# First six projection jobs on an input centred by rows but not normalised: tokens loaded by quarters, the norm made during later jobs

## The chip, the cores and the metric

The kernel runs on one NeuronCore of one Trainium2 chip. The metric is device time in microseconds (us) of one execution; the kernel before was timed three times. Engines are named as the profile names them: PE (TensorE, matrix products), PEld (its weight loads), DVE (VectorE), ACT (ScalarE), POOL (GpSimd) and SP (SyncE, which here only issues DMAs). "Span" is the time from the first to the last instruction in the profiled execution.

## The reference, cut to what matters

One layer of a hybrid decoder, in fp32, on 304 token rows: 16 learned meta tokens, 256 prompt tokens and 8 samples of 4 tokens. The change touches the input LayerNorm and the first projections behind it.

```python
def _layernorm(x, g, b):
    mu = jnp.mean(xf, axis=-1, keepdims=True)
    var = jnp.mean(jnp.square(xf - mu), axis=-1, keepdims=True)
    return (xf - mu) * lax.rsqrt(var + LN_EPS) * g + b

xp = _layernorm(jnp.concatenate([meta, x_prompt], axis=1), ln0_g, ln0_b)
xs = _layernorm(x_sample, ln0_g, ln0_b)
...
proj = x @ w_in            # 2048 x 7168: q, zf, v, g (8 heads of 128), three conv groups of 1024
... # HGRN2 recurrence on q, zf, v, gated by g; short gated convolution on the other three
mix = jnp.concatenate([o_a, y_b], axis=-1) @ w_o
h = _layernorm(ALPHA * x + mix, ln1_g, ln1_b)
ff = (jax.nn.silu(h @ w_gate) * (h @ w_up)) @ w_down
out = _layernorm(ALPHA * h + ff, ln2_g, ln2_b)
```

## The kernel before, in words

All activations stand transposed: 128 channels on the partitions, the 304 tokens (T; L = 288 without the meta tokens) along the free axis, 16 blocks of channels. Every fp32 operand of a product is split into a rounded part `hi` and a remainder `lo`, and each product is three matmuls: hi·xh, hi·xl, lo·xh.

Weights come in *pieces* of 512 KB (4 blocks of 128 rows by 256 columns). A *job* is one projection to 256 output channels: 4 pieces, 16 steps k, and in each step 2 x 3 matmuls into two PSUM banks (lines 184 to 186, in `run_job`). SP loads a piece into one of five raw buffers (line 117); ACT casts it to `hi` (line 74) and DVE subtracts to get `lo` (line 75); early in the program the same two instructions carry line 56, that of a helper which keeps an engine's instructions in the order in which they are written. Five pairs of hi and lo buffers exist, so piece n can be split once PE is through with piece n-5, and SP can load into a raw buffer once the piece before it in that buffer is split.

The jobs run in a fixed order: z, v, q, g of heads 0 and 1 (jobs 1 to 4), the same of heads 2 and 3 (jobs 5 to 8), a convolution block (three jobs), and so on; then the output projection and the feed-forward. Between the steps `tick` emits a little of the side work: taking finished banks out of PSUM (`evac`), the recurrence (`scan_head`), the convolution. The scheduler of the framework then sets the order of each engine's queue; every engine runs its own queue strictly in order.

At the start all of the input is loaded (lines 325 to 332: meta tokens, then halves of the rows), then the first weight pieces. The statistics of the three row tiles (128, 128 and 48 rows) are made on DVE and ACT, the rows are normalised, PE transposes them block by block (`turn`, line 387, xT), and `settle` applies gain and bias and splits into xh and xl. Four blocks are prepared before job 1 (bank zb) begins; the others follow in its steps. Job 2 (bank vb) is the first without such work.

Of the kernel before, what the change touches and what calls it, by code (L numbers as in the profile page):

```python
# [10 lines left out]
F32 = mybir.dt.float32  # L11
# [8 lines left out]
H = 8  # L20
# [20 lines left out]
LEAD = 4  # L41
# [18 lines left out]
def hybrid_step(ctx: ExitStack, tc: tile.TileContext, io):  # L60
# [10 lines left out]
    vec, act, pe = (InOrder(tc, e) for e in (nc.vector, nc.scalar, nc.tensor))  # L71
# [40 lines left out]
    def load_ahead(i):  # L112
        while state["dma"] < min(len(pieces), i + AHEAD_DMA):
# [14 lines left out]
    def split_next(first=False):  # L128
# [4 lines left out]
        if first:  # L133
            for k in range(n):
                act.copy(out=hi[:, k], in_=raw[:, k])
                nc.gpsimd.tensor_tensor(out=lo[:, k], in0=raw[:, k], in1=hi[:, k].bitcast(F32), op=ALU.subtract)
        elif p < 8:
            split(raw, hi, lo, vec, act)
        else:
            split(raw, hi, lo)  # L140
        splits[p] = (hi, lo)
        state["split"] += 1

# [5 lines left out]
    def tick():  # L149
        for q in lanes.values():  # L150
# [18 lines left out]
    def run_job(rhs, n, name):  # L169
# [5 lines left out]
        for i, k in enumerate(ks):  # L175
# [5 lines left out]
            for m in range(nm):  # L181
                cs = slice(m * P, (m + 1) * P)
                o = banks[m][:, :n]
                nc.tensor.matmul(o, hi[:, i % kb, cs], xh, start=(i == 0), stop=False)  # L184
                nc.tensor.matmul(o, hi[:, i % kb, cs], xl, start=False, stop=False)  # L185
                nc.tensor.matmul(o, lo[:, i % kb, cs], xh, start=False, stop=(i == nk - 1))  # L186
# [9 lines left out]
    prow0 = const.tile([NP0, P], F32, name="prow0")  # L196
    prows = const.tile([NP1, P], F32, name="prows")
    pvec = const.tile([P, NP0 + NP1], F32, name="pvec")
    crows = const.tile([3 * H, P], F32, name="crows")
# [14 lines left out]

    ident = const.tile([P, P], F32, name="ident")
# [85 lines left out]
    def rstd_tok(pool, mv, n, w, tag):  # L301
# [6 lines left out]
        nc.scalar.activation(out=t[:n], in_=v[:n], func=AF.Sqrt)  # L308
        nc.vector.reciprocal(out=r[:n], in_=t[:n])
# [8 lines left out]


    with tc.tile_pool(name="x0", bufs=1) as x0p, tc.tile_pool(name="x0w", bufs=3) as x0w:  # L320
        rows = [P, P, T - 2 * P]
        xts = [x0p.tile([P, D], F32, name=f"xt{i}") for i in range(3)]
        HD = D // 2
        nc.scalar.preload_act_table_set("sqrt_and_others")
        nc.sync.dma_start(out=xts[0][:NMETA], in_=io["meta_tokens"])
        nc.sync.dma_start(out=xts[0][NMETA:, :HD], in_=io["x_prompt"][0, : P - NMETA, :HD])
        nc.sync.dma_start(out=xts[2][:NMETA], in_=io["x_prompt"][0, 2 * P - NMETA :])
        nc.sync.dma_start(out=xts[2][NMETA : NMETA + NS], in_=io["x_sample"].rearrange("b t d -> (b t) d"))
        nc.sync.dma_start(out=xts[0][NMETA:, HD:], in_=io["x_prompt"][0, : P - NMETA, HD:])
        for c in range(2):  # L330
            cs = slice(c * HD, (c + 1) * HD)
            nc.sync.dma_start(out=xts[1][:, cs], in_=io["x_prompt"][0, P - NMETA : 2 * P - NMETA, cs])
        load_rows(nc.sync, prow0, 0, ("ln0_g", "ln0_b"))
# [6 lines left out]
        nc.gpsimd.memset(epsb, LN_EPS)  # L340

        junk = x0p.tile([T - 2 * P, D], F32, name="junk")

        def bn(i, st, c):
            vec.bn_stats(out=st[:, c], in_=xts[i][:, c * 512 : (c + 1) * 512])

        def stat_tiles(i):
            return [x0p.tile([P, n], F32, name=f"{tag}{i}") for tag, n in (("mv", 2), ("v", 1), ("r", 1), ("t", 1), ("nmr", 1))]

        def rstd(i):  # L350

            n = rows[i]
            mv, v, r, t, nmr = (x[:n] for x in sts[i])
            act.activation(out=t, in_=mv[:, 1:2], func=AF.Sqrt, bias=epsb[:n])
            vec.tensor_scalar_add(out=v, in0=mv[:, 1:2], scalar1=LN_EPS)
            yield
            vec.reciprocal(out=r, in_=t)
            yield
            vec.scalar_tensor_tensor(out=t, in0=r, scalar=v, in1=r, op0=ALU.mult, op1=ALU.mult)
            yield  # L360
            vec.tensor_scalar(out=t, in0=t, scalar1=-0.5, scalar2=1.5, op0=ALU.mult, op1=ALU.add)
            yield
            vec.tensor_mul(out=r, in0=r, in1=t)
            yield
            vec.scalar_tensor_tensor(out=nmr, in0=mv[:, 0:1], scalar=-1.0, in1=r, op0=ALU.mult, op1=ALU.mult)

        def together(*gens):
            for _ in zip_longest(*gens):
                pass

        def norm_rows(i, c, eng):
            n = rows[i]
            mv, _, r, _, nmr = (x[:n] for x in sts[i])
            x = xts[i][:n, c * 512 : (c + 1) * 512]
            if eng is vec:
                eng.tensor_scalar(out=x, in0=x, scalar1=mv[:, 0:1], scalar2=r, op0=ALU.subtract, op1=ALU.mult)
            else:
                eng.activation(out=x, in_=x, func=AF.Identity, scale=r, bias=nmr)
# [3 lines left out]
        def turn(k, tiles):  # L382
            if k not in xT:
                xT[k] = bank("xT")
            for i in tiles:
                n = rows[i]
                nc.tensor.transpose(xT[k][:, i * P : i * P + n], xts[i][:n, k * P : (k + 1) * P], ident[:n, :n])

        xfs = {}

        def settle(k):

            if k < NB:
                b = xT.pop(k)
                xf = x0w.tile([P, T], F32, tag="xf", name="xf", bufs=4)
                vec.tensor_scalar(out=xf, in0=b[:, :T], scalar1=pcol("ln0_g", k), scalar2=pcol("ln0_b", k), op0=ALU.mult, op1=ALU.add)
                act.copy(out=xh[:, k], in_=xf)
                xfs[k] = xf
            if k:
                eng = vec if k % 4 == 1 else nc.gpsimd  # L400
                eng.tensor_tensor(out=xl[:, k - 1], in0=xfs.pop(k - 1), in1=xh[:, k - 1].bitcast(F32), op=ALU.subtract)

        sts = [stat_tiles(i) for i in range(3)]
        bn0, bn1 = (x0p.tile([P, 4, 6], F32, name=f"bn{i}") for i in range(2))
        s2, mv2, x2 = x0p.tile([P, 2], F32, name="s2")[: rows[2]], sts[2][0][: rows[2]], xts[2][: rows[2]]
        act.activation(out=junk, in_=x2, func=AF.Identity, accum_out=s2[:, 0:1])
        for c in range(3):
            bn(0, bn0, c)
        vec.tensor_scalar(out=mv2[:, 0:1], in0=s2[:, 0:1], scalar1=1.0 / D, scalar2=None, op0=ALU.mult)
        vec.tensor_scalar(out=s2[:, 0:1], in0=s2[:, 0:1], scalar1=-1.0 / D, scalar2=None, op0=ALU.mult)  # L410
        bn(0, bn0, 3)
        vec.bn_aggr(out=sts[0][0], in_=bn0)
        together(rstd(0))
        act.activation(out=junk, in_=x2, func=AF.Square, bias=s2[:, 0:1], accum_out=s2[:, 1:2])
        for c in range(2):
            norm_rows(0, c, act)
        for c in range(4):
            bn(1, bn1, c)
        vec.tensor_scalar(out=mv2[:, 1:2], in0=s2[:, 1:2], scalar1=1.0 / D, scalar2=None, op0=ALU.mult)
        vec.bn_aggr(out=sts[1][0], in_=bn1)  # L420
        together(rstd(1), rstd(2))
        pb = bank("pb", "main")
        nc.tensor.transpose(pb[:, :NP0], prow0, ident[:NP0, :NP0])
# [775 lines left out]
```

## Time and profile before

| | us |
|---|---|
| median of 3 runs | 1412.75 (1412.15 to 1412.88) |
| profiled execution, its own time | 1411.89 |
| its span | 1410.2 |
| PE busy in it | 1382.0 (98%) |
| DVE, ACT, POOL busy | 831.2, 587.9, 115.6 |
| first matmul of job 1 | 20.15 |
| first matmul of job 2 | 45.35 |
| first matmul of job 7 | 114.69 |

A row of the time view reads: start, duration, engine, line, operation, output<-inputs, shape, count, and in brackets the idle time of the engine ahead of it with what ended it. Rows that run back to back overlap a little in their durations, since matmul ends are modelled and vector instructions are pipelined; the distance from start to start is what an instruction costs its engine. The profiled time is 1.7 us longer than the span.

### The profile page before, as it was taken

Reading aid. Unit: us, or ns where it says so; the run is one execution under the profiler, and the core shown is the slowest. Engines: PE = TensorE matmul, PEld = TensorE weight load, DVE = VectorE, ACT = ScalarE, POOL = GpSimd, SP = SyncE. Lnnn points to the kernel's source line nnn. Section 1 sums busy time; section 2 is a strip of 40 time slices with the busy share of each in tenths; the row PEclk is TensorE's granted clock in tenths of the full one; section 3 lists DMA queues with packets and bytes.
Section 4 is the critical chain, followed back from the end, with each engine's and each line's share of the span. In section 5 each row is a group of like instructions: output and inputs, shape, how many; then the busy total and the mean of one; then the engine's idle time right before and its main releaser. Section 6 shows DMA issues by size and latency. Waiting matters only on the chain.

```text
span 1410.2 us, 24922 instructions
## 1 busy us (share of the span) xinstructions
PE 1382.0 (98%) x10311; PEld 1365.6 (97%) x10311; DVE 831.2 (59%) x1342; ACT 587.9 (42%) x823; POOL 115.6 (8%) x174
## 2 busy tenths in 40 slices
PE   5999999999999999999999999999999999999996
PEld 4999999999999999999999999999999999999995
DVE  6756676876676888966444444444444444465444
ACT  5645544555443444434333333333333333343330
POOL 5201121111000332000000000000000000020000
PEclk9999999999999999999999999999999999999998
DMA  6655655555545554555555555555555555565541
GB/s 188 208 162 162 181 167 168 173 150 169 170 148 165 161 161 151 177 165 165 165 165 165 167 152 167 166 167 181 165 165 165 165 165 165 165 196 165 157 128 68
DMA packets 223858, 231.12 MB, mean 164 GB/s; under 512 B 7756, under 2 KB 219576, under 8 KB 223546
## 3 DMA queue, kind: packets, MB, share of 16 engines
q1 hardware_dynamic: 220240, 218.54, 50.9%
q0 software_dynamic: 3312, 10.72, 2.7%
q8 instruction: 81, 1.33, 0.4%
q10 hardware_dynamic: 192, 0.26, 0.1%
q14 instruction: 33, 0.27, 0.1%
HBM read 222.34 MB, written 7.15 MB: 163 GB/s over the span
## 4 chain that ended last, share of the span: by engine, by line
PE 98%; DVE 1%; POOL 1%; issue 0%; DVEq 0%; ACT 0%; POOLq 0%
PE u L184 7%; PE g L184 7%; PE wd L186 7%; PE g L185 7%; PE u L185 7%; PE wd L185 7%; PE g L186 7%; PE u L186 7%; PE wd L184 7%; PE wo L186 2%; PE wo L185 2%; PE wo L184 2%; PE zb L184 2%; PE zb L185 1%; PE zb L186 1%; PE vb L184 1%
## 5 line engine op out<-in xcount | busy, mean ns | idle before, releaser
L75 DVE TENSOR_TENSOR lo<-raw,hi 128x1024 fp32r<-128x1024 f32 (+1 forms) x408 | 501.7, 1231 | 476.5 <-ACT hi L74 476.0
L74 ACT CAST hi<-raw 128x1024 fp32r<-128x1024 f32 (+1 forms) x408 | 421.3, 1033 | 635.5 <-PE u L185 162.6
L185 PE MATMUL wd<-al,hi 128*128 128x288 f32 x704 | 207.9, 295 | 0.0
L184 PE MATMUL wd<-ah,hi 128*128 128x288 f32 x704 | 207.8, 295 | 0.0
L186 PE MATMUL wd<-ah,lo 128*128 128x288 f32 x704 | 207.8, 295 | 0.0
L184 PE MATMUL g<-ygh,hi 128*128 128x288 f32 (+1 forms) x452 | 134.0, 296 | 0.0
L185 PE MATMUL u<-ygl,hi 128*128 128x288 f32 (+1 forms) x452 | 133.9, 296 | 0.0
L185 PE MATMUL g<-ygl,hi 128*128 128x288 f32 (+1 forms) x452 | 133.9, 296 | 0.0
L184 PE MATMUL u<-ygh,hi 128*128 128x288 f32 (+1 forms) x452 | 133.8, 296 | 0.0
L186 PE MATMUL g<-ygh,lo 128*128 128x288 f32 (+1 forms) x452 | 133.6, 296 | 0.0
L186 PE MATMUL u<-ygh,lo 128*128 128x288 f32 (+1 forms) x452 | 133.6, 296 | 0.0
L185 PEld LDWEIGHTS wd<-al,hi 128*128 128x128 f32 x704 | 132.3, 188 | 0.0
L186 PEld LDWEIGHTS wd<-ah,lo 128*128 128x128 f32 x704 | 132.2, 188 | 0.0
L184 PEld LDWEIGHTS wd<-ah,hi 128*128 128x128 f32 x704 | 132.1, 188 | 0.1
L186 PEld LDWEIGHTS u<-ygh,lo 128*128 128x128 f32 x452 | 85.4, 189 | 0.0
L184 PEld LDWEIGHTS g<-ygh,hi 128*128 128x128 f32 x452 | 85.3, 189 | 0.1
L186 PEld LDWEIGHTS g<-ygh,lo 128*128 128x128 f32 x452 | 85.3, 189 | 0.0
L185 PEld LDWEIGHTS g<-ygl,hi 128*128 128x128 f32 x452 | 85.3, 189 | 0.1
L185 PEld LDWEIGHTS u<-ygl,hi 128*128 128x128 f32 x452 | 85.3, 189 | 0.0
L184 PEld LDWEIGHTS u<-ygh,hi 128*128 128x128 f32 x452 | 85.3, 189 | 0.0
L186 PE MATMUL wo<-mh,lo 128*128 128x288 f32 x256 | 75.9, 296 | 0.0
L185 PE MATMUL wo<-ml,hi 128*128 128x288 f32 x256 | 75.6, 295 | 0.0
(391 smaller groups left out, 3132.3 us busy)
## 6 DMA issues: line engine op xcount, KB each, us to landing
raw<-in_w_in SPq DMA_DIRECT2D x112, 512.0 KB, 3.7
raw<-in_w_gate SPq DMA_DIRECT2D x88, 512.0 KB, 3.6
raw<-in_w_up SPq DMA_DIRECT2D x88, 512.0 KB, 3.6
raw<-in_w_down SPq DMA_DIRECT2D x79, 512.0 KB, 3.6
raw<-in_w_o SPq DMA_DIRECT2D x32, 512.0 KB, 3.6
s<-in_state_hgrn POOLq DMA_DIRECT2D x8, 512.0 KB, 5.5
out<-sn POOLq DMA_DIRECT2D x8, 512.0 KB, 4.4
raw<-in_w_down SPq DMA_DIRECT2D x15, 256.0 KB, 2.8
```

What stands on the lines that cost most here:

```text
L74: a.copy(out=hi, in_=src)
L75: v.tensor_tensor(out=lo, in0=src, in1=hi.bitcast(F32), op=ALU.subtract)
L184: nc.tensor.matmul(o, hi[:, i % kb, cs], xh, start=(i == 0), stop=False)
L185: nc.tensor.matmul(o, hi[:, i % kb, cs], xl, start=False, stop=False)
L186: nc.tensor.matmul(o, lo[:, i % kb, cs], xh, start=False, stop=(i == nk - 1))
```

## The change

The first six jobs (z, v, q, g of heads 0 and 1, z and v of heads 2 and 3) no longer read the normalised input. They read `mixh` and `mixl`: the rows minus a rough centre (the mean of the row's first 128 values), transposed, times the gain, split. Two more columns at the end of that operand carry the gain and the bias themselves, so that each job also gives W·gain and W·bias. `evac_raw` then makes the projection of the normalised input: bank times the row's 1/std, plus W·gain times minus mean/std, plus W·bias. The buffers `mixh` and `mixl` are those that later hold the mixer's output.

* Loads: the tokens come in four quarters of columns, and after each quarter SP loads one weight piece; a quarter of the short row groups (sample rows, the prompt's end, meta tokens) is issued by ACT, the remaining three quarters of them by POOL; the gains by POOL, ahead of everything.
* The third row tile is padded with zero rows, so that its transposes from block 4 on are 128 wide and not 48.
* PE gets three products of the identity at the start and one after the first transposes; their results are not used.
* The centring of the later quarters, formerly part of the normalising on DVE and ACT, lies partly on POOL. Row statistics (`bn_stats`, `row_sums`) are made inside job 1 and closed after it in `first_norm`, which also spreads 1/std and -mean/std over the partitions by six small products (rb).
* `normed_input` makes the normalised xh, xl, which job 7 and all later jobs read: for each of 16 blocks one add and one multiply on POOL, an affine copy on ACT, an add on DVE, a cast on ACT and a subtraction on DVE. It runs as a side lane during jobs 2 to 6.
* The look-ahead of the splits is 0 for job 1's pieces and then grows to 3, one piece at a time.

The queue of SP, the program's first rows. Before (xt_103, xt_104, xt_105 are the three row tiles):

```order
L325 DMA xt_103<-in_meta_tokens 16x2048
L326 DMA xt_103<-in_x_prompt 112x1024
L327 DMA xt_105<-in_x_prompt 16x2048
L328 DMA xt_105<-in_x_sample 32x2048
L329 DMA xt_103<-in_x_prompt 112x1024
L332 DMA xt_104<-in_x_prompt 128x1024 x2
L211 DMA prow_67<-in_ln_g 16x128
L211 DMA prow_67<-in_ln_b 16x128
L117 DMA raw<-in_w_in 128x4x256 x112
```

and in the change (xt_111, xt_112 are the first two row tiles, the third is not loaded by SP):

```order
L57 DMA xt_111<-in_x_prompt 112x512
L57 DMA xt_112<-in_x_prompt 128x512
L57 DMA raw<-in_w_in 128x4x256
L57 DMA xt_111<-in_x_prompt 112x512
L57 DMA xt_112<-in_x_prompt 128x512
L57 DMA raw<-in_w_in 128x4x256
L57 DMA xt_111<-in_x_prompt 112x512
L57 DMA xt_112<-in_x_prompt 128x512
L57 DMA raw<-in_w_in 128x4x256
```

The first weight piece stood behind nine loads and now stands behind two of SP's.

DVE's queue from the split (lo) of piece 11 to that of piece 12, the last of job 3 and the first of job 4, before (pieces are counted from 0):

```order
L75 TENSOR_TENSOR lo<-raw,hi 128x1024
L541 SCALAR_TENSOR_TENSOR c<-c,loglb,w_1043 128x304
L543 SCALAR_TENSOR_TENSOR b<-reset,c 128x304
L509 CAST vs_1000<-vT 128x2x32
L550 TENSOR_SCALAR el<-b 128x16
L510 TENSOR_TENSOR vs_1000<-vT,vs_1000 128x2x32
L551 TENSOR_TENSOR el<-b 128x256
L552 TENSOR_TENSOR el<-b 128x32
L556 TENSOR_TENSOR w_1100<-b 128x256
L75 TENSOR_TENSOR lo<-raw,hi 128x1024
```

and in the change, from the split of piece 10 to just behind that of piece 12:

```order
L76 TENSOR_TENSOR lo<-raw,hi 128x1024
L516 TENSOR_TENSOR xf<-xf,xw 128x304
L76 TENSOR_TENSOR lo<-raw,hi 128x1024
L76 TENSOR_TENSOR xl<-xf,xh 128x304
L516 TENSOR_TENSOR xf<-xf,xw 128x304
L797 COPY u<-vT_504 128x2
L798 TENSOR_TENSOR vT<-vT_504,xr 128x304
L76 TENSOR_TENSOR xl<-xf,xh 128x304
L76 TENSOR_TENSOR lo<-raw,hi 128x1024
L799 SCALAR_TENSOR_TENSOR vT<-xnm,u,vT 128x304
```

Between the splits now stand the norm (xf, xl, with POOL's work in xf ahead of each) and the correction of the banks (u, vT); the recurrence's rows (c, b, el) come some pieces later.

The diff, cut to its core:

```diff
-LEAD = 4
+NXC = 4
+NRAW = 6
+WARM = 3
...
     def ensure(i):
         load_ahead(i)
-        while state["split"] < min(state["dma"], i + 1 + min(AHEAD_SPLIT, max(1, i - 1))):
+        while state["split"] < min(state["dma"], i + 1 + min(AHEAD_SPLIT, max(0, i + 1 - NXC))):
...
+    load_rows(pool, prow0, 0, ("ln0_g", "ln0_b"))
...
+        for dst, src in small:
+            act.dma_start(out=dst[:, :XC], in_=src[:, :XC])
+        tc.keep_in_program_order(nc.scalar.preload_act_table_set("natural_log_exp_and_others"))
+        vec.memset(xts[2][NS : 2 * NS, XC:], 0.0)
+        vec.memset(xts[2][2 * NS :, XC:], 0.0)
+        for c in range(NXC):
+            cs = slice(c * XC, (c + 1) * XC)
+            sync.dma_start(out=xts[0][NMETA:, cs], in_=xin[: P - NMETA, cs])
+            sync.dma_start(out=xts[1][:, cs], in_=xin[P - NMETA : 2 * P - NMETA, cs])
+            load_to(c + 1)
         load_ahead(0)
+        for dst, src in small:
+            pool.dma_start(out=dst[:, XC:], in_=src[:, XC:])
...
+        for _ in range(WARM):
+            idle_product(4)
...
+        def row_centre(i):
+            m = cen[: rows[i], i : i + 1]
+            vec.tensor_reduce(out=m, in_=xts[i][: rows[i], :P], op=ALU.add, axis=mybir.AxisListType.X)
+            vec.tensor_scalar(out=m, in0=m, scalar1=-1.0 / P, scalar2=None, op0=ALU.mult)
...
         def settle(k):
+            b, g = xT.pop(k)[:, :T], pcol("ln0_g", k)
+            act.activation(out=mixh[:, k, :T], in_=b, func=AF.Copy, scale=g)
+            vec.scalar_tensor_tensor(out=mixl[:, k, :T], in0=b, scalar=g, in1=mixh[:, k, :T].bitcast(F32),
+                                     op0=ALU.mult, op1=ALU.subtract)
...
+        row_centre(0)
+        centre(0, 0, vec)
+        row_centre(2)
+        centre(2, 0, act)
+        row_centre(1)
+        centre(1, 0, vec)
         pb = bank("pb", "main")
+        pe.transpose(pb[:, :NP0], prow0, ident[:NP0, :NP0])
         vec.tensor_copy(out=pvec[:, :NP0], in_=pb[:, :NP0])
+        turn(0)
+        turn(1)
+        idle_product(2)
         settle(0)
...
         def first_rhs(k):
+            c, i = divmod(k, 4)
+            if i == 0:
+                for j in (2, 3):
+                    turn(k + j)
+                for j in (2, 3):
+                    settle(k + j)
+                if k == 0:
+                    for j, eng in ((0, vec), (1, act), (2, pool)):
+                        centre(j, 1, eng)
+                    load_rows(pool, prows, NP0, ("b_f", "lb_param", "gnorm_g", "ln1_g", "ln1_b"))
...
+            if i == 2:
+                if k < 8:
+                    for j in range(3):
+                        centre(j, c + 2, pool)
+                split_next()
...
+            if k in (13, 15):
+                next(sums)
+            return mixh[:, k], mixl[:, k]
...
+    def first_norm():
+        for i in range(2):
+            nc.vector.bn_aggr(out=mv[:, i], in_=bns[i])
+        r, nmr = rstd_tok(sp, mv, P, 3, "x")
+        yield 5
...
+    def normed_input():
+        for k in range(NB):
...
+            nc.gpsimd.tensor_tensor(out=x, in0=mixh[:, k, :T].bitcast(F32), in1=mixl[:, k, :T].bitcast(F32), op=ALU.add)
+            yield 1
+            nc.gpsimd.tensor_tensor(out=x, in0=x, in1=xr, op=ALU.mult)
+            nc.scalar.activation(out=w, in_=xnm, func=AF.Identity, scale=pcol("ln0_g", k), bias=pcol("ln0_b", k))
+            yield 1
+            nc.vector.tensor_add(out=x, in0=x, in1=w)
+            yield 1
+            split(x, xh[:, k], xl[:, k])
+            yield 1
...
+    def evac_raw(n, banks, out, tag, fn):
+        yield LAG
+        for j in range(2):
...
+            nc.vector.tensor_copy(out=u, in_=banks[j][:, n : n + 2])
+            nc.vector.tensor_mul(out=t, in0=banks[j][:, :n], in1=xr[:, T - n :])
+            nc.vector.scalar_tensor_tensor(out=t, in0=xnm[:, T - n :], scalar=u[:, 0:1], in1=t, op0=ALU.mult, op1=ALU.add)
+            fn(j, t, t, u[:, 1:2])
...
+    def project(t0, out, tag, fn):
+        raw = state["job"] < NRAW
+        if state["job"] == NRAW:
+            flush("norm")
+        n = T - t0
+        banks = run_job(centred_rhs(t0), n + 2, tag) if raw else run_job(xrhs(t0), n, tag)
+        side("evac", (evac_raw if raw else evac)(n, banks, out, tag, fn))
```

More of the change, by code (lines that the diff above doesn't have):

```diff
@@ L112, in load_ahead, with load_to @@
     def load_ahead(i):
-        while state["dma"] < min(len(pieces), i + AHEAD_DMA):
+        load_to(i + AHEAD_DMA)
+    def load_to(end):
+        while state["dma"] < min(len(pieces), end):
             p = state["dma"]
@@ L124, in ensure, with split_next, split_steps @@
         load_ahead(i)
-        while state["split"] < min(state["dma"], i + 1 + min(AHEAD_SPLIT, max(1, i - 1))):
+        while state["split"] < min(state["dma"], i + 1 + min(AHEAD_SPLIT, max(0, i + 1 - NXC))):
             split_next()
-    def split_next(first=False):
+    def split_next():
+        for _ in split_steps(state["split"] >= 8):
+            pass
+    def split_steps(whole):
         p = state["split"]
@@ L132, in split_next @@
         raw = blocks(raws.pop(p), p)
[L133 to L140, printed above, removed]
         splits[p] = (hi, lo)
         state["split"] += 1
+        if whole:
+            split(raw, hi, lo)
+            return
+        if p:
+            split(raw, hi, lo, vec, act)
+            return
+        for k in range(n):
+            split(raw[:, k], hi[:, k], lo[:, k], vec, act)
+            yield
     lanes = {}
@@ L149, in tick @@
     def tick():
-        for q in lanes.values():
+        for q in list(lanes.values()):
             if not q[0]:
@@ L195, in hybrid_step @@
     NP1 = 2 * NB + 4 * H
-    prow0 = const.tile([NP0, P], F32, name="prow0")
-    prows = const.tile([NP1, P], F32, name="prows")
+    s0x = ExitStack()
+    x0p = s0x.enter_context(tc.tile_pool(name="x0", bufs=1, side="right"))
+    prow0 = x0p.tile([NP0, P], F32, name="prow0")
     pvec = const.tile([P, NP0 + NP1], F32, name="pvec")
-    crows = const.tile([3 * H, P], F32, name="crows")
     cvec = const.tile([P, 3 * H], F32, name="cvec")
@@ L307, in rstd_tok @@
         nc.vector.tensor_scalar_add(out=v[:n], in0=mv[:n, :, 1], scalar1=LN_EPS)
-        nc.scalar.activation(out=t[:n], in_=v[:n], func=AF.Sqrt)
-        nc.vector.reciprocal(out=r[:n], in_=t[:n])
+        nc.scalar.activation(out=t[:n], in_=v[:n], func=AF.Ln)
+        nc.scalar.activation(out=r[:n], in_=t[:n], func=AF.Exp, scale=-0.5)
         newton(r[:n], v[:n], t[:n])
@@ L317, in hybrid_step @@
     xl = xp.tile([P, NB, T], F32R, name="xl")
-    with tc.tile_pool(name="x0", bufs=1) as x0p, tc.tile_pool(name="x0w", bufs=3) as x0w:
+    mixp = s1.enter_context(tc.tile_pool(name="mixp", bufs=1))
+    mixh = mixp.tile([P, NB, T + 2], F32R, name="mh")
+    mixl = mixp.tile([P, NB, T + 2], F32R, name="ml")
+    mh, ml = mixh[:, :, :L], mixl[:, :, :L]
+    mv = xp.tile([P, 3, 2], F32, name="mv")
+    bns = [xp.tile([P, NXC, 6], F32, name=f"bn{i}") for i in range(2)]
+    s2t = xp.tile([P, 3], F32, name="s2t")
@@ L321, in hybrid_step @@
+    with s0x:
         rows = [P, P, T - 2 * P]
+        prows = x0p.tile([NP1, P], F32, name="prows")
+        crows = x0p.tile([3 * H, P], F32, name="crows")
         xts = [x0p.tile([P, D], F32, name=f"xt{i}") for i in range(3)]
[L323 to L333, printed above, removed]
+        XC = D // NXC
+        xin = io["x_prompt"][0]
+        small = ((xts[2][NMETA : NMETA + NS], io["x_sample"].rearrange("b t d -> (b t) d")),
+                 (xts[2][:NMETA], xin[2 * P - NMETA :]), (xts[0][:NMETA], io["meta_tokens"]))
@@ L340, in hybrid_step @@
[L340 to L350, printed above, removed]
-            n = rows[i]
-            mv, v, r, t, nmr = (x[:n] for x in sts[i])
-            act.activation(out=t, in_=mv[:, 1:2], func=AF.Sqrt, bias=epsb[:n])
-            vec.tensor_scalar_add(out=v, in0=mv[:, 1:2], scalar1=LN_EPS)
+        warm = bank("warm", "main")
@@ new lines, in centre, with turn @@
+        def centre(i, c, eng):
+            n = rows[i]
+            x, m = xts[i][:n, c * XC : (c + 1) * XC], cen[:n, i : i + 1]
+            if eng is act:
+                eng.activation(out=x, in_=x, func=AF.Identity, bias=m)
+            else:
+                eng.tensor_scalar(out=x, in0=x, scalar1=m, scalar2=None, op0=ALU.add)
+        xT = {}
+        def turn(k):
+            xT[k] = bank("xT")
+            for i in (0, 2, 1):
+                n = rows[i] if k * P < XC else P
+                pe.transpose(xT[k][:, i * P : i * P + n], xts[i][:n, k * P : (k + 1) * P], ident[:n, :n])
@@ L356, in rstd @@
             yield
[L357 removed]
+            act.activation(out=junk, in_=x2, func=AF.Square, bias=s2[:, 2:3], accum_out=s2[:, 1:2])
+            vec.tensor_scalar(out=m2[:, 1:2], in0=s2[:, 1:2], scalar1=1.0 / D, scalar2=None, op0=ALU.mult)
             yield
[L359 to L361 removed]
@@ L362, in rstd @@
[L362 to L378, printed above, removed]
@@ L380, in hybrid_step @@
-        xT = {}
[L382 to L421, printed above, removed]
+        row_centre(0)
@@ L432, in hybrid_step @@
+        turn(1)
+        idle_product(2)
         settle(0)
+        gb0 = pvec[:, :NP0].rearrange("p (a b) -> p b a", b=NB)
+        split(gb0, mixh[:, :, T:], mixl[:, :, T:], vec, act)
+        first_split = split_steps(False)
+        next(first_split)
         settle(1)
-        norm_rows(1, 1, vec)
-        norm_rows(2, 1, act)
-        settle(2)
-        settle(3)
+        for _ in first_split:
+            pass
+        sums = row_sums()
         def first_rhs(k):
-            c = k // 2 + 2
-            if k % 2 == 0 and c < 4:
-                norm_rows(0, c, act)
-                norm_rows(1, c, vec)
-                norm_rows(2, c, vec)
-            if k + LEAD < NB:
-                turn(k + LEAD, (0, 1, 2))
-            if k + LEAD <= NB:
-                settle(k + LEAD)
-            return xh[:, k], xl[:, k]
@@ new lines, in first_rhs @@
+            if i == 2:
[3 more added lines that the diff above has]
+                split_next()
+                if k + 2 < NB:
+                    for j in (2, 3):
+                        turn(k + j)
+                    for j in (2, 3):
+                        settle(k + j)
+            if i % 2:
+                vec.bn_stats(out=bns[i // 2][:, c], in_=xts[i // 2][:, c * XC : (c + 1) * XC])
+            if k in (13, 15):
+                next(sums)
@@ L473, in hybrid_step, with centred_rhs @@
     nc.gpsimd.memset(vtm, 0.0)
+    xr, xnm = (sp.tile([P, T], F32, tag="cc", name=n, bufs=2) for n in ("xr", "xnm"))
+    def first_norm():
[3 more added lines that the diff above has]
+        yield 5
+        for dst, src in ((xr, r), (xnm, nmr)):
+            b = bank("rb")
+            for i in range(3):
+                nc.tensor.matmul(b[:, i * P : i * P + rows[i]], src[:, i : i + 1].broadcast_to([P, P]), ident[:, : rows[i]],
+                                 start=True, stop=True)
+            nc.scalar.copy(out=dst, in_=b[:, :T])
+        side("norm", normed_input())
+        yield 1
+    def normed_input():
+        for k in range(NB):
+            x = sp.tile([P, T], F32, tag="y", name="xf", bufs=2)
+            w = sp.tile([P, T], F32, tag="up", name="xw")
+            nc.gpsimd.tensor_tensor(out=x, in0=mixh[:, k, :T].bitcast(F32), in1=mixl[:, k, :T].bitcast(F32), op=ALU.add)
[6 more added lines that the diff above has]
+            split(x, xh[:, k], xl[:, k])
+            yield 1
+    def centred_rhs(t0):
+        return lambda k: (mixh[:, k, t0:], mixl[:, k, t0:])
     def xrhs(t0):
```

73 lines of the change are left out of this document (39 added, 34 removed).

## The prediction

> **What bounds the kernel now.** I read the page first, then what TensorE waited for, then its time view around job 1, where the change works.
>
> ```profile
> span 1410.2 us, 24922 instructions
> PE 1382.0 (98%) x10311; PEld 1365.6 (97%) x10311; DVE 831.2 (59%) x1342; ACT 587.9 (42%) x823; POOL 115.6 (8%) x174
> PE   5999999999999999999999999999999999999996
> PE 98%; DVE 1%; POOL 1%; issue 0%; DVEq 0%; ACT 0%; POOLq 0%
> ```
>
> ```profile
> PE pb L423 <- DMA prow<-in_ln_b: 13.2, 1, 13.2
> ```
>
> Only the first slice of 35 us and the last are not full, the chain of waits lies 98% on PE, and PE's one long wait is for the first loads. So the time is PE's work plus what PE loses at the start and the end; what the change is worth is read from where PE stands when job 7 begins, behind which both kernels do the same work. PE's time view:
>
> ```profile
> 20.15 0.85 PE L184 MATMUL zb<-xh,hi 128*128 128x304 f32 x2
> ...
> 23.60 0.46 PE L185 MATMUL zb<-xl,hi 128*128 128x304 f32 x1
> 23.85 0.46 PE L186 MATMUL zb<-xh,lo 128*128 128x304 f32 x1
> ...
> 24.87 0.90 PE L387 MATMUL xT<-ident,xt 128*128 128x128 f32 x3
> 25.70 0.62 PE L184 MATMUL zb<-xh,hi 128*128 128x304 f32 x1
> ...
> 28.20 0.41 PE L184 MATMUL zb<-xh,hi 128*128 128x304 f32 x1
> 28.72 0.30 PE L184 MATMUL zb<-xh,hi 128*128 128x304 f32 x1
> 28.86 0.30 PE L185 MATMUL zb<-xl,hi 128*128 128x304 f32 x1
> ...
> 31.08 0.40 PE L184 MATMUL zb<-xh,hi 128*128 128x304 f32 x1
> 32.02 0.57 PE L387 MATMUL xT<-ident,xt 128*128 128x128 f32 x3
> 32.52 0.55 PE L184 MATMUL zb<-xh,hi 128*128 128x304 f32 x2
> ...
> 40.78 0.27 PE L454 MATMUL pb<-ident,prows 64*128 64x64 f32 x1
> 42.21 0.41 PE L185 MATMUL zb<-xl,hi 128*128 128x304 f32 x1
> 45.35 0.30 PE L184 MATMUL vb<-xh,hi 128*128 128x304 f32 x1
> ...
> 114.69 0.29 PE L184 MATMUL qb<-xh,hi 128*128 128x288 f32 x1
> ```
>
> Four things stand here. Job 1 begins at 20.15, the input being loaded and normalised by then. Until 28.20 a product costs 0.253 us from start to start, then 0.139: PE ran at half rate for its first 8.05 us of dense work. At full rate a step with its three transposes takes 1.44 us. Job 2 begins at 45.35 and job 7 at 114.69, 69.34 us later. In those 69 us DVE has room:
>
> ```profile
> 45.35:114.67 69.32, 69.32 (x516) 68.60 (x515) 42.83 (x71) 34.54 (x53) 5.13 (x4) 1.00 0.67 199
> ```
>
> (the columns are length, then busy time of PE, PEld, DVE, ACT, POOL, the granted clock, DMA share and GB/s). DVE 42.8, ACT 34.5, POOL 5.1 of 69.3.
>
> **The change, step by step.** *First product.* What has to land first sets it (rows of the time view, of the DMA issues with the us to landing, of the windows).
>
> ```profile
> 6.06 1.29 DVE L56 BATCH_NORM_STATS2 bn<-xt 128x6 f32<-128x512 f32 x2 [6.06 <-DMA xt<-in_x_prompt]
> 16.87 0.53 DVE L56 TENSOR_SCALAR xt<-xt,mv,r 128x512 f32<-128x512 f32 x1
> prows<-in_b_f POOLq DMA_DIRECT2D x1, 4.0 KB, 5.2
> prows<-in_lb_param POOLq DMA_DIRECT2D x1, 8.0 KB, 5.8
> 0.00:5.00 5.00, 0.00 (x0) 0.00 (x0) 0.00 (x0) 1.28 (x1) 3.96 (x13) 1.00 0.70 163
> 5.00:10.00 5.00, 0.00 (x0) 0.00 (x0) 1.76 (x3) 1.97 (x2) 4.48 (x28) 1.00 0.93 241
> ```
>
> Before, 128 + 448 KB had landed at 6.06. Now the second quarter tile is complete after 224 + 256 + 128 KB, so about 6.0; sum, scale and centre on DVE (0.3, 0.15, 0.53) end at 7.0. The gains come by POOL in 5.2 and 5.8 us from issues at 0.8 and 1.5: 7.3, and through PE and a copy at 7.8. The first weight piece ends at 1120 KB, by the windows' rates (163 GB/s x 5 us = 815 KB, then 241) at 6.3 and a completion later, about 8. PE: six transposes at half rate from 7.55 (0.24 each: the three at 24.87 take 0.83, with a gap for the 48-row shape, which falls away), the idle product, six more, then the first product at 10.6; ACT and DVE have its operands by 9.8. Bounds: 9.3 (the second six transposes cost nothing) and 13.5 (the quarters land as late as half tiles did). I take **10.6**, 9.55 earlier.
>
> *Job 1.* Half rate lasts 8.05 us there and I keep it: four steps of 1.52 and six transposes of 1.45 take PE to 18.1. The quarters are ready: SP's second pair is complete at 1.6 MB, by the windows at 8.3 plus a completion, POOL's part (issued behind DVE's memsets at about 4, 5.2 to 7 us) by 12, needed at 13.7. DVE's centring of the second quarter waits for POOL's meta rows, and behind it stand statistics and the lo of piece 1, not needed before 18. On POOL seven small loads (0.5 each) stand ahead of the third quarter's centring, which ends at 19; PE transposes it at 20.7. Then twelve steps at 6 x 0.139 = 10.0 and five groups of six transposes at 0.157 (0.50 for the three at 32.02, less the other shape) = 4.7: the last product ends at 32.8. DVE has to do 12 of these 14.7 us (ten mixl of 0.46, three splits, six statistics), so it keeps up, barely. The small transposes (40.78 to 42.21, less two products) add 1.3: job 2 begins at **34.1, gain 11.25**. Bounds 31.5 and 38 (POOL's six centres of about 1 us each late by a group).
>
> *PE's new work*: six small products for rb, 0.9; two columns in 304 on 480 products of jobs 2 to 6, 0.4. The three identity products lie before 7 us, where PE waits anyway; without that cover they would cost under 3.
>
> *Behind job 1* ACT's queue carries, ahead of the cast of piece 5, what it did at leisure before:
>
> ```profile
> 8.03 1.91 ACT L56 ACTIVATE junk<-xt 48x2048 f32<-48x2048 f32 x1 [5.94 <-DMA xt<-in_x_sample]
> 11.64 1.99 ACT L56 ACTIVATE junk<-xt,s 48x2048 f32<-48x2048 f32 x1
> 43.10 1.28 ACT L273 ACT_TABLE_LOAD   x1
> ```
>
> From its last mixh at 30.4: sum 2.1, cast of piece 4 1.04, squares 2.2, table 1.28, the two chains of Exp and Ln with DVE between 0.9, cast of piece 5 1.04 = 38.95, its lo on DVE 40.1. PE wants it at 37.6: **2.5 lost**. The rb products stand in PE's queue just ahead of that step and wait for the same chain on DVE, which ends at 39.0; job 2's last three pieces wait behind them. Bounds 0.5 and 4.
>
> *Jobs 2 to 6, DVE.* The largest cost. How POOL's two-input operations meet DVE is shown in the output-projection stage:
>
> ```profile
> 467.05 0.45 DVE L811 SCALAR_TENSOR_TENSOR yc<-xh,wo 128x288 f32<-128x288 f32 x1
> 469.39 0.45 DVE L825 TENSOR_TENSOR yc<-yc,lnc 128x288 f32<-128x288 f32 x1
> 469.76 0.45 DVE L813 SCALAR_TENSOR_TENSOR yc<-xl,yc 128x288 f32<-128x288 f32 x1
> 469.98 0.89 POOL L838 TENSOR_TENSOR lns<-lns,yc 128x288 f32<-128x288 f32 x1 [1.19 <-DVE yc L825]
> 470.13 1.83 DVE L75 TENSOR_TENSOR lo<-raw,hi 128x1024 fp32r<-128x1024 f32 x1
> 470.89 1.74 POOL L839 TENSOR_TENSOR lnq<-lnq,lq 128x288 f32<-128x288 f32 x1
> 471.88 1.06 DVE L825 TENSOR_TENSOR yc<-yc,lnc 128x288 f32<-128x288 f32 x1
> 476.04 1.21 DVE L75 TENSOR_TENSOR lo<-raw,hi 128x1024 fp32r<-128x1024 f32 x1
> ```
>
> A split takes 1.21 alone and 1.83 when POOL adds, the next operation 1.06 for 0.45: each POOL operation of 288 columns takes 0.61 from DVE, 0.64 at 304. An operation that reads PSUM (line 811) passes untouched. DVE's queue, from piece 5's lo at 39.0: pieces 5 to 9 in a row until 45.0 (1.14 each, a little waiting for ACT); then up to piece 24, job 7's first: 15 splits 17.1; 15 adds xf and 15 subtractions xl at 0.39 (0.37 between the starts of 469.39 and 469.76, scaled) 11.7; the banks' correction (copy 0.1, multiply 0.40, add 0.44, z one more 0.42) 10.0; head 0's recurrence 8.8. Sum 47.6. One POOL product of 1024 columns, as in the row below, 1.7. Thirty POOL operations meet it, 0.64 each; some fall on operations that read PSUM (about 15% of DVE's time), so 16.3.
>
> ```profile
> L564 DVE TENSOR_TENSOR el<-k,el 128x16 f32<-128x16 f32 x1 | 1.9, 1911 | 0.0
> ```
>
> 45.0 + 47.6 + 1.7 + 16.3 = **110.6**. PE would want it at 34.1 + 69.3 + 1.3 + 2.5 = 107.2. So PE loses 3.4 more, spread over jobs 5 to 7, and job 7 begins at 110.6, not 114.69. Bounds: no loss (107.2), every POOL operation met in full (113.5). Behind job 7 the norm is over, DVE's rows per four pieces sum to 10 us against PE's 13, and nothing more is lost. ACT has 46 us of work in these 66.
>
> Sum: 1411.89 - 4.1 = 1407.8 for the profiled execution; the median of the runs shown lies 0.86 above it: **1408.7**.
>
> **The rivals.** *DVE keeps up*: POOL's work falls into DVE's pauses. For it: DVE is 26 us idle there before. Against: the sum leaves only 62.2 - 49.3 = 12.9 us of room for 19.2. It decides if under two thirds of the POOL operations meet DVE. Job 7 at 107.2, gain 7.5: **1405.3**.
>
> *The lock is longer*, the slower side: each POOL operation keeps DVE out for its whole length, not for 0.61. POOL's add ran from 470.13, when DVE's operation ended, to 470.87; scaled to 304 columns 0.78. All thirty meeting DVE: 45.0 + 49.3 + 23.4 = 117.7, 3.0 later than before: **1415.8**. It is slower than before from 0.68 us per operation on. For it: DVE's queue is full, so every operation waits. Against: the two rows with 0.61. The Trainium skill says this in its page SBUF — State Buffer, section SBUF: two separate sides: whichever starts first holds the shared port pair for the whole instruction and the other fully blocks. The rows agree that DVE blocks, and put it at 0.61 of 0.74.
>
> *The clock stays at half rate through job 1*, because PE's new start has gaps (after its identity products, before each group of transposes). From 18.1: 72 products x 0.253 + 30 transposes x 0.235 = 25.3 and not 14.7; everything behind is 10.6 later: job 7 at 121.2, **1419.3**. For it: it took 8.05 us before, not fewer. Against: that start had gaps too, and rose.
>
> **How the numbers follow.** Forecast 0.50, DVE keeps up 0.23, the longer lock 0.18, half rate 0.09. The likeliest case's own range, from job 1's bounds and those of DVE's sum, is 1405.5 to 1412.5. A measurement of this kernel tells 0.2% (2.8 us) from no change, so faster is below 1409.9 and slower above 1415.6. Of the forecast 0.28 is faster and 0.22 the same; of the lock 0.06 the same and 0.12 slower. Faster 0.28 + 0.23 = 0.51; same 0.22 + 0.06 = 0.28; slower 0.12 + 0.09 = 0.21. The range for 8 in 10 takes in keeping up and most of the lock: 1404 to 1417.
>
> **What would show it.** First product of job 1 near 10.6, and its rate halving its cost near 18; job 2 at 34; a wait of PE for piece 5's lo of some 2 us; DVE without a pause from 45 to 110, its splits at 1.8 where POOL works; job 7 near 110.6. If splits stay at 1.2 beside POOL, or DVE shows pauses of several us in jobs 4 to 6, the third step is wrong and the time is lower; if job 2 begins after 38, the first is.

## The result, and the profile after

The changed kernel takes 1420.26 us (median of 5 runs, 1417.42 to 1420.65) where the kernel before takes 1412.75 (5 runs, 1412.15 to 1414.05): 1.0049 times as long, 95% interval 1.0034 to 1.0064. It is slower by 7.5 us. The prediction said 1408.7 and gave slower 0.21. The profiled execution took 1420.08.

The page of the kernel after, in the same rows as before:

```profile
span 1418.4 us, 25107 instructions
PE 1389.0 (98%) x10331; PEld 1371.5 (97%) x10331; DVE 867.7 (61%) x1404; ACT 601.0 (42%) x853; POOL 151.0 (11%) x202
PE   7988999999999999999999999999999999999996
```

PE's first slice is fuller than before (7, not 5), but the next two are 9 and 8, then 8. What PE waited for up to 160 us (sum, times, longest):

```profile
PE kv L681 <- ACT kdt L665: 4.2, 1, 4.2
PE xT L57 <- POOL xt L57: 3.8, 3, 3.2
PE z L196 <- DVE lo L76: 3.6, 2, 3.1
PE warm L57 <- POOL ident masks.py:199: 3.3, 1, 3.3
PE xT L57 <- DVE xt L57: 1.4, 1, 1.4
PE rb L500 <- ACT hi L57: 1.0, 1, 1.0
```

Before, the one long wait was the 13.2 us for the first loads. It is gone, and in its place stand three waits of 3 to 4 us (kv, xT and z; the 3.3 us of the row "warm" lie ahead of the identity products, before the job has work). PE's time view shows where they fall:

```profile
11.81 0.39 PE L57 MATMUL zb<-mh,hi 128*128 128x306 f32 x1
12.04 0.30 PE L57 MATMUL zb<-ml,hi 128*128 128x306 f32 x1
12.18 0.31 PE L57 MATMUL zb<-mh,lo 128*128 128x306 f32 x1
...
20.85 0.33 PE L57 MATMUL xT<-ident,xt 128*128 128x128 f32 x1 [0.33 <-POOL xt L57]
24.40 1.27 PE L57 MATMUL xT<-ident,xt 128*128 128x128 f32 x5 [3.22 <-POOL xt L57]
...
25.73 0.46 PE L57 MATMUL zb<-ml,hi 128*128 128x306 f32 x1
25.98 0.46 PE L57 MATMUL zb<-mh,lo 128*128 128x306 f32 x1
...
37.99 0.41 PE L194 MATMUL vT<-mh,hi 128*128 128x306 f32 x1
...
94.91 0.41 PE L196 MATMUL z<-mh,lo 128*128 128x306 f32 x1 [3.15 <-DVE lo L76]
...
116.44 1.04 PE L681 MATMUL kv<-vt,kdt 128*128 128x128 f32 x4 [4.15 <-ACT kdt L665]
...
122.64 0.30 PE L194 MATMUL q<-xh,hi 128*128 128x288 f32 x1
```

Job 1 begins 8.3 us earlier than before (11.81 against 20.15), job 2 7.4 us earlier (37.99 against 45.35), job 7 8.0 us later (122.64 against 114.69). From job 7 to the end of the span it is 1295.7 us here and 1295.5 before: all of the loss lies between job 2 and job 7. Behind each of the three waits (behind the second from 1.3 us after its end) the products come 0.254 us apart (25.73 to 25.98) for about 3.4 us, and then 0.14 again: PE ran at half rate. Jobs 2 to 6 in one row of the windows:

```profile
37.99:122.50 84.51, 75.70 (x527) 73.91 (x526) 81.97 (x150) 54.38 (x93) 40.99 (x39) 0.96 0.54 161
```

They take 84.5 us instead of 69.3. PE is idle in 8.8 of them (the waits above), and busy 6.4 longer: half rate twice, the six small products, two columns. DVE is busy in 82.0 of 84.5 us (42.8 of 69.3 before) and POOL in 41.0 (5.1).

### The profile page after: what moved, and what is told of

Read it like the earlier page. It is cut to its first block, busy times and chain, and to the rows that moved or that the text cites. A ratio compares the mean times of both kernels' runs of the same rounds, so it can differ in the third digit from the quotient of the medians.

```text
span 1418.4 us, 25107 instructions
## 1 busy us (share of the span) xinstructions
PE 1389.0 (98%) x10331; PEld 1371.5 (97%) x10331; DVE 867.7 (61%) x1404; ACT 601.0 (42%) x853; POOL 151.0 (11%) x202
## 4 chain that ended last, share of the span: by engine, by line
PE 93%; DVE 4%; ACT 1%; POOL 1%; issue 1%; DMA 1%; DVEq 0%; ACTq 0%; POOLq 0%
PE u L194 7%; PE g L194 7%; PE wd L196 7%; PE g L195 7%; PE u L195 7%; PE wd L195 7%; PE g L196 7%; PE u L196 7%; PE wd L194 7%; PE wo L195 2%; PE wo L194 2%; PE wo L196 2%; PE xb L194 1%; PE cb L194 1%; PE gbb L194 1%; PE cb L195 1%
```

## The experiments

All medians are to be read beside the change's 1420.3; the kernel before measured 1412.0 to 1412.7 with them.

**Centring off POOL.** In job 1:

```diff
-                if k < 8:
-                    for j in range(3):
-                        centre(j, c + 2, pool)
...
+                elif k < 12:
+                    for j, eng in ((0, vec), (2, act), (1, act)):
+                        centre(j, c + 1, eng)
```

> The centring of the third and fourth quarter of the input goes from POOL (1.56 to 1.63 us a tile, behind seven small loads) to DVE (one tile of each quarter, 0.49) and ACT (two tiles, 0.72 each). Theory A, that POOL's centring made TensorE wait 3.2 us in job 1 and that this wait put the clock back to half rate for 3.4 us: no wait over 1 us at the third quarter, no half rate behind it, job 2 at 33.3 and not 37.99. As DVE's queue begins earlier by as much, the whole gains about as much: 1415.8 for the kernel with the change of 1420.3. Theory B, that DVE alone bounds jobs 2 to 6 and its queue does not begin earlier (it waits for weight pieces or for ACT's chain behind job 1): job 2 at 33 to 34, job 7 still near 122, 1420.

1415.22 us (11 runs, 1413.81 to 1417.33). What the edit takes away, in the time view and the groups of POOL up to 125 us in the kernel after:

```profile
14.07 1.57 POOL L57 TENSOR_SCALAR xt<-xt,cen 48x512 f32<-48x512 f32 x1 [9.29 <-DMA xt<-in_x_prompt]
...
19.22 9.75 POOL L57 TENSOR_SCALAR xt<-xt,cen 128x512 f32<-128x512 f32 x6
...
L57 POOL TENSOR_SCALAR xt<-xt,cen 128x512 f32<-128x512 f32 x4 | 6.2, 1561 | 0.0
```

Six tiles took 9.75 us: five of them 1.55 to 1.58 each, and the third, beside a split of DVE, 2.05. So the third quarter's three were through at 24.3. POOL began them only at 19.22: its centre of the second quarter waited for a load until 14.07, and the seven small loads stand between. With DVE and ACT in POOL's place PE does not wait for the third quarter (0.55 us for the fourth), and job 2 begins at 35.37:

```profile
35.37 0.41 PE L194 MATMUL vT<-mh,hi 128*128 128x306 f32 x1
```

That is not the 33.3 expected, mostly because in this execution PE ran at half rate from 16.0 to 19.4, behind a wait of 1.7 us for the second quarter. In the execution of the kernel with eight raw jobs (below), which is alike in job 1, it did not, and job 2 began at 32.55. The whole gained 5.0 us, so an earlier job 2 is passed on (theory A); the waits in jobs 5 and 6 stayed (2.6 and 4.2 us).

**Norm left out, first try.** The call of `normed_input` was taken out and two zero fills of `xh` and `xl` put on POOL behind `make_constants`.

> The 16 steps that make the normalised input in jobs 2 to 6 are left out (POOL's add and multiply, ACT's line and cast, DVE's add and subtraction); POOL fills the operands of the later jobs with zeros instead, so from job 7 on other numbers are multiplied in the same time. Theory A, that these steps load DVE (about 0.78 for its own two operations and 1.28 for POOL's two, 16 times 2.06 = 33 us) and so make TensorE wait in jobs 5 and 6: no wait over 1 us and no half rate between job 2 and job 7; job 7 at 38.0 + 69.3 + 2.5 = 109.8 and not 122.5, the whole 1408. Theory B, that the correction of the banks and the recurrence of head 0, which stay, make DVE late by themselves: job 7 at 116 or later, 1414 or more.

1414.73 us (10 runs), job 7 at 118.2: inside theory B's numbers, but not by its cause. PE waited 5.5 us, at rb in job 2; DVE and POOL in the time view of this kernel:

```profile
37.39 1.22 DVE L57 TENSOR_TENSOR lo<-raw,hi 128x1024 fp32r<-128x1024 f32 x1 [0.73 <-ACT hi L57]
...
40.19 4.88 DVE L318 TENSOR_SCALAR xv<-mv 128x3 f32<-128x3 f32 x1
...
36.48 4.18 POOL L470 MEMSET xh<- 128x4864 f32 x1
40.59 4.17 POOL L471 MEMSET xl<- 128x4864 f32 x1
```

The fill itself did it: a DVE operation on three columns stood until POOL's second fill was over. In jobs 3 to 6 no wait was left, but this run does not price the norm; a later one does.

**Norm's add and multiply on DVE.**

```diff
-            nc.gpsimd.tensor_tensor(out=x, in0=mixh[:, k, :T]..., in1=mixl[:, k, :T]..., op=ALU.add)
+            nc.vector.tensor_tensor(out=x, in0=mixh[:, k, :T]..., in1=mixl[:, k, :T]..., op=ALU.add)
             yield 1
-            nc.gpsimd.tensor_tensor(out=x, in0=x, in1=xr, op=ALU.mult)
+            nc.vector.tensor_tensor(out=x, in0=x, in1=xr, op=ALU.mult)
```

> POOL's add and multiply of each of the 16 steps are done by DVE. Theory A, that each of POOL's operations on 304 columns keeps DVE out for 0.64 us, more than the 0.39 that DVE takes to do it: DVE gains 32 times 0.25 = 8 us by doing 32 operations more; the waits of 3.15 and 4.15 in jobs 5 and 6 and the half rate behind them shrink or go; job 7 at 112 to 115, the whole 1410 to 1413. Theory B, that POOL's operations mostly passed beside DVE's and the lateness came from DVE's own work: 12.5 us more on DVE, job 7 near 130 and the whole 1428 or more.

1410.98 us (11 runs, 1408.64 to 1412.29): 9.3 us less, and below the kernel before (0.9988, 0.9979 to 0.9996). Groups of DVE from 40 to 122 us, then POOL's up to 125, in the kernel after:

```profile
L76 DVE TENSOR_TENSOR lo<-raw,hi 128x1024 fp32r<-128x1024 f32 x20 | 28.3, 1420 | 0.0
L76 DVE TENSOR_TENSOR xl<-xf,xh 128x304 fp32r<-128x304 f32 x16 | 10.6, 662 | 1.9 <-ACT xh L75 1.8
...
L513 POOL TENSOR_TENSOR xf<-xf,xr 128x304 f32<-128x304 f32 x16 | 18.7, 1173 | 2.1 <-ACT xr L502 1.0
L511 POOL TENSOR_TENSOR xf<-mh,ml 128x304 f32<-128x304 f32 x16 | 16.3, 1018 | 27.0 <-DVE xl L76 27.0
```

and DVE's in this one:

```profile
L76 DVE TENSOR_TENSOR lo<-raw,hi 128x1024 fp32r<-128x1024 f32 x23 | 28.0, 1216 | 0.9 <-ACT hi L75 0.9
...
L513 DVE TENSOR_TENSOR xf<-xf,xr 128x304 f32<-128x304 f32 x16 | 7.5, 468 | 0.0
L76 DVE TENSOR_TENSOR xl<-xf,xh 128x304 fp32r<-128x304 f32 x16 | 7.5, 468 | 2.2 <-ACT xh L75 2.2
```

A split is back at 1.22 (from a mean of 1.42), a subtraction at 0.47 (from 0.66). From the start of piece 5's split to the end of the norm's last subtraction DVE was busy 72.8 us in the change (42.60 to 117.44) and 67.9 here (40.84 to 110.87), though here it did 30 operations more at 0.39 from start to start, 11.6 us (the other two lie ahead of this stretch). Of the rest of its work it did about 0.2 us less, two small operations of the next head. So the 30 on POOL had cost DVE 4.9 + 11.6 - 0.2 = 16.3 us, 0.54 each. Handing them to POOL took more of DVE than doing them there.

**Idle products in the wait.** Ahead of the third quarter's transposes:

```diff
+                if k == 6:
+                    for _ in range(3):
+                        idle_product(4)
```

> Three idle products of the identity (0.82 each at full rate) are put on TensorE ahead of the transposes of the third quarter, into the wait of 3.22 us for POOL; they write a bank that nothing reads. Theory A, that a pause of about 3 us is what puts the clock back to half rate: the pause is then under 1 us, no half rate behind it (products from 25 on at 0.14 and not at 0.254), job 2 at 36.4 and not 37.99, up to 1.5 us less in the whole: 1418.8. Theory B, that the clock falls whatever TensorE does there: job 2 at 38.0 to 38.5, 1420.3.

1418.43 us (5 runs, 1417.25 to 1419.23).

```profile
22.07 2.73 PE L57 MATMUL warm<-ident 128*128 128x512 f32 x6
24.64 1.09 PE L57 MATMUL xT<-ident,xt 128*128 128x128 f32 x6
...
25.71 0.30 PE L57 MATMUL zb<-ml,hi 128*128 128x306 f32 x1
25.85 0.30 PE L57 MATMUL zb<-mh,lo 128*128 128x306 f32 x1
```

The quarter comes no earlier, but the products behind it run 0.14 apart at once and job 2 begins at 36.99, 1.0 us earlier; at job 7 it is 0.8 (121.81). The medians differ by 1.8, but the ranges overlap for the most part. That fits theory A, but one execution does not show it: in those of the norm on DVE and of the kernel without identity products at the start, waits of 2.8 and 3.0 us for the same quarter were not followed by half rate either.

**Norm left out, second try.** In `normed_input` only two ACT casts of `xnm` a step remain:

```diff
+            nc.scalar.copy(out=xh[:, k], in_=xnm)
+            yield 2
+            nc.scalar.copy(out=xl[:, k], in_=xnm)
+            yield 2
```

> The norm's arithmetic is left out once more, without the zero fill on POOL that held DVE: in each of the 16 steps ACT alone writes the two operands of the later jobs, as casts of one and the same row tile (0.44 each, in place of the 0.64 and 0.44 that it did there), so from job 7 on other numbers are multiplied in the same time; DVE's two and POOL's two operations of a step are gone. Theory A, that these load DVE until TensorE waits in jobs 5 and 6: no wait over 1 us there, job 7 at 38.0 + 69.3 + 2.5 = 109.8 and not 122.5, the whole 1408. Theory B, that what stays (the banks' correction, the recurrence of head 0, the place of its matrix products) makes TensorE wait by itself: job 7 at 115 or later, 1413 or more.

1407.68 us (4 runs, 1406.69 to 1408.08), job 7 at 110.7. What PE still waits for between 38 and 200 us is one row:

```profile
PE rb L500 <- ACT hi L57: 0.6, 1, 0.6
```

The norm's arithmetic therefore makes all the waits of jobs 5 and 6, and with their half rate costs 12.6 us. The banks' correction and head 0, which stay, fit in DVE's room.

**Both edits** (centring on DVE and ACT, add and multiply on DVE).

> Both edits that gained alone: the centring of the third and fourth quarter on DVE and ACT, and the norm's add and multiply on DVE. Theory A, that the two losses stand one behind the other (PE's late start of job 2, then DVE's late queue): the gains add, 1411.0 less 5.0 = 1406. Theory B, that DVE's sum of 67 us from piece 5's lo on bounds job 7 whatever starts before, or that the centring on DVE and ACT only moves the wait inside job 1: 1409 to 1411, no better than the norm on DVE alone.

1406.71 us (5 runs, 1406.27 to 1409.05): 0.9963 of the kernel before (0.9951 to 0.9976), 13.6 less than the change as it was. The gains add to 14.3 and nearly all of it came. Jobs 2 to 6 and their waits:

```profile
34.40:109.80 75.40, 72.16 (x527) 70.81 (x526) 73.17 (x174) 54.63 (x93) 5.66 (x7) 1.00 0.55 169
```

```profile
PE ktb L645 <- DVE kp L614: 1.7, 1, 1.7
PE rb L500 <- ACT hi L57: 0.8, 1, 0.8
PE vsb L567 <- DVE vs L559: 0.7, 1, 0.7
```

DVE is still full (73.2 of 75.4 us), but PE loses only 3.2 us to it.

**Keys' products later.** One number, ahead of `kv = bank("kv")`:

```diff
-        yield 1
+        yield 8 if h == 0 else 1
```

> One number: in head 0's recurrence the products that read the transposed keys (the wait of 4.15 us in job 6) stand eight steps of the job later in TensorE's queue instead of one, so 42 products of job 6, whose weight pieces are split by then (the last at 109.1), are no longer queued behind them. Theory A, that the wait is one of place, DVE's lateness reaching TensorE through ACT's queue, where the copy of the keys stands behind the norm's cast: no wait over 2 us there, no half rate behind it; job 7 near 117 to 118.5 and not 122.5, the whole 1415 to 1417. Theory B, that DVE's queue bounds job 7 by its pieces in any order: the wait comes back at the first piece of job 7 or at a later product of head 0, job 7 or the next job loses as much, 1419.5 to 1420.5.

1416.78 us (6 runs, 1414.99 to 1418.3), 3.5 less, at the upper end of what theory A gave.

```profile
114.02 0.29 PE L194 MATMUL q<-xh,hi 128*128 128x288 f32 x1
...
116.73 0.61 PE L681 MATMUL kv<-vt,kdt 128*128 128x128 f32 x4
```

The wait of 4.15 us is gone, and job 7 begins at 114.02 with DVE unchanged (piece 24 split at 114.4). Theory A had it at 117 to 118.5. It is 8.6 us earlier there than in the change, but only 4.7 are left at the end of the profiled execution: 1.1 us of products now lie behind that point, and PE waits 2.2 us more behind it than in the change, 1.7 of them for the keys of a later head; the other 0.6 is not accounted for. (The products behind the keys in job 6 are 24; the expectation's 42 was a miscount.) In the change these products waited for ACT, and ACT for DVE:

```profile
115.18 0.46 DVE L516 TENSOR_TENSOR xf<-xf,xw 128x304 f32<-128x304 f32 x1
...
115.67 0.44 ACT L75 CAST xh<-xf 128x304 fp32r<-128x304 f32 x1 [2.20 <-DVE xf L516]
116.03 0.37 ACT L665 COPY kdt<-ktb 128x256 f32<-128x256 f32 x1
```

The copy of the keys needed nothing from the norm; it stood behind the norm's cast in ACT's queue.

**No identity products at the start** (`WARM = 0`).

> The three identity products ahead of the first transposes are left out (nothing reads what they write). Theory A, that they are why job 1 began at full rate, and that the wait for the third quarter hides what the rate costs before it: first products at 0.254 for 3.4 or 6.9 us, TensorE at the third quarter's transposes 1.5 to 3 us later and waiting that much less; job 2 still at 37.5 to 38.5, the whole within 1 us of 1420.3. Theory B, that the rate in job 1 moves job 2 one for one: job 2 at 39.5 to 41, 1422 to 1423.5.

1420.09 us (4 runs, 1418.89 to 1421.32). Job 2 and the whole came as theory A had them:

```profile
14.66 0.46 PE L57 MATMUL zb<-ml,hi 128*128 128x306 f32 x1
14.91 0.46 PE L57 MATMUL zb<-mh,lo 128*128 128x306 f32 x1
...
25.46 0.76 PE L57 MATMUL xT<-ident,xt 128*128 128x128 f32 x5 [3.01 <-POOL xt L57]
...
37.49 0.41 PE L194 MATMUL vT<-mh,hi 128*128 128x306 f32 x1
```

Job 1 begins 2.5 us later, at half rate until 17.5, and the wait for POOL's third quarter hides it. That wait is hardly shorter than in the change (3.0 against 3.2), since the quarter itself came 1.1 us later in this execution; but no half rate followed it. So the early rate bought nothing that these runs show, in part by chance.

**Spreading the norm over eight raw jobs**, on top of both edits (`NRAW = 8`, two of the four `yield 1` in `normed_input` made `yield 2`), and **the transposes of the keys later**, on top of both edits (`yield 8 if h == 0 else 3` ahead of `ktb`).

> The kernel with both edits (centring off POOL, the norm's add and multiply on DVE), with eight raw jobs instead of six: each of the 16 steps of the norm now takes six steps of a job instead of four, and the query and gate banks of the second head pair are corrected too (four banks, about 0.95 us of DVE each). Theory A, that DVE's full queue from 50 to 110 us is all that is left to lose there: its load per job falls from about 12.5 to 10.5 us in jobs 3 to 6, TensorE's waits of 1.7 and 0.7 us go, and the whole is 1404 to 1405.5 where both edits alone gave 1406.7. Theory B, that the load only moves behind job 7, where the recurrences of heads 1 and 2 fill DVE: the same waits come later, 1406.5 to 1408.5.

> The kernel with both edits, and head 0's transposes of its keys eight steps of the job behind the products before them instead of three (one number). Theory A, that the wait of 1.7 us that is left for these keys is one of place: it goes, 1405 where both edits alone gave 1406.7. Theory B, that DVE is late by an amount that some later product pays in any order: 1406.5 to 1407.

1408.0 us (8 runs, 1406.04 to 1409.72) and 1408.68 (7 runs, 1407.33 to 1410.05): no better than both edits. The first is what theory B gave, the second lies above both theories. With eight raw jobs the wait for the keys is gone from job 6 and one comes in job 8:

```profile
135.50 0.69 PE L645 MATMUL ktb<-ident,kp 128*128 128x128 f32 x2 [2.00 <-DVE kp L614]
```

With the later transposes head 0 no longer waits for its keys. In its place PE waits at a later product of head 0, in job 7,

```profile
PE sb L686 <- DVE ats_b L672: 1.0, 1, 1.0
```

and 1.6 us in all for the keys of later heads, where both edits alone have no wait behind job 7 until the end. In these two runs, with DVE full, a wait that was moved was paid somewhere else; where the keys' products were moved in the change itself, 3.5 us of it stayed gained.

## Why the prediction was wrong, step by step

* **First product.** 11.81 and not 10.6, within its bounds. From there PE ran at full rate, where half rate until 18.1 was forecast. PE came to the third quarter's transposes at 20.5, where 20.7 was forecast, but by luck: the full rate made up for the later start and for 1.6 us of waits for the second quarter.
* **Job 1: wrong, two sizes.** The step that failed is "POOL's six centres of about 1 us each", held to be in time, and with it POOL's part of the loads, forecast "by 12". That part was there at 14.07, and the four centres that end with the third quarter took 6.7 us instead of 4 (the seven loads 3.6, as forecast). So the third quarter was ready at 24.3 and not 19, where PE wanted it at 20.5. The wait cost 3.2 us, and the half rate behind it about 1.0 more at job 2. Job 2 began at 37.99, just inside the bound of 38, not at 34.1; without that centring on POOL the change takes 1415.2.
* **Behind job 1.** The wait for piece 5 and the chain of Exp and Ln was 1.05 us, where 2.5 stood.
* **DVE's sum was right.** 71.6 us from the start of piece 5's split to the end of piece 24's were forecast (38.95 to 110.6), 72.1 were measured, 2.0 of them idle, which the sum did not have. POOL's operations cost DVE 0.54 each on the mean, where 0.64 for 85% of them stood, which is 0.54 as well, and a split that met one took 1.86, where 1.8 stood. Piece 24 was split at 114.7 instead of 110.6 because the queue began 3.6 us later.
* **Job 7 at the end of DVE's queue: wrong, and the largest error.** Job 7 came 12.0 us after its forecast, 4.1 of them with the end of DVE's queue and 7.9 behind it. The sum took the split of piece 24 to be the only thing PE wants from DVE, "3.4 more, spread over jobs 5 to 7". PE also stands in order behind everything of head 0 that goes through DVE or ACT. It waited 3.15 us for piece 19 at 91.8 and 4.15 at 112.3 for the keys, with 24 products of job 6 behind them whose piece was split; job 7 began 7.9 us after piece 24 was ready. With the keys' products eight steps later and DVE's queue as it was, job 7 did begin when piece 24 was split, 114.0, as the step had assumed.
* **The rate behind a wait was left out.** Half rate was weighed for job 1's start alone. Here it came back after each of the three long waits, some 3.4 us at half rate each time. Such a stretch loses half its length, so by this estimate a wait of 3 us was worth up to 4.7.
* **The rivals.** DVE did not keep up. The longer lock gave 1415.8, nearer the measured time, for the wrong reason: the mean price of a POOL operation was 0.54, below the 0.68 from which it decides. Half rate all through job 1 did not come.

The idea of the change was sound: job 2 begins 7.4 us earlier, and with two placements changed the kernel takes 1406.7, 0.37% less than before. It was slower as made because it put work on POOL that was late there in job 1 and took DVE's time in jobs 2 to 6.

## What to carry to other kernels

When an engine's queue is full, look at every instruction in the bound engine's queue that depends on it, directly or through a third engine's queue, and not only at the last one: the first that is late stops all that is behind it. Price work that goes to POOL by what it takes from DVE as well as by its own time; here 0.54 us of DVE for an operation that DVE does in 0.39. And count a wait of PE of about 3 us or more with the half rate that follows.

## What the runs showed of the hardware

* **The rate after a pause.** In the first 200 us every pause of PE of 3.2 us or more between products in these runs (3.22, 3.3, 4.15, 4.2, 5.5, 5.6, 5.6) was followed by a granted clock of 0.50, for 3.4 us or twice that. Pauses of 1.7 to 3.15 were followed by it in some executions and not in others: 1.7, 2.6, 2.8 and 3.15 each at least once were and at least once were not. The rate in the first us of job 1 differed as well between executions of kernels that are alike there, full in the change's and half until 17 us in another. The Trainium skill describes this in its page TensorE: Matmul & The Clock Gate, section Part 1: The HAM clock gate: the rate follows from a free-running window of about 3.4 us. The lengths of 3.4 and 6.8 us agree, and so does the chance in between.
* **POOL and DVE hold each other up both ways.** A POOL operation on 128x304 took 1.02 and 1.17 us beside a full DVE, where 0.78 was scaled from the rows before. In job 1 a centre on POOL and a split on DVE that met took 2.05 and 1.91, where 1.56 and 1.21 are usual. The page SBUF — State Buffer of the Trainium skill (section SBUF: two separate sides) says that a POOL fill, which reads nothing, does not meet a DVE operation with two inputs, but meets one in a two-port performance mode. The run with the two fills agrees in the first, since the split passed at 1.22; the TENSOR_SCALAR on three columns stood 4.88 us, but one on a single column passed at 0.15, and no run here shows which of them was in such a mode.
* **POOL is slow at a simple add of a column.** 1.56 us for 128x512, and 1.57 for 48x512, where DVE took 0.49 and ACT 0.72.
